# The input and forget gates of an mLSTM: float32 matmuls of 32 columns in four column groups instead of split matmuls of 100 columns

## The chip, the cores and the metric

The kernel runs on one core of a Trainium2 chip. The metric is the device time of one execution in microseconds (us); lower is better. The time before is the median of three runs.

## The reference, cut to what matters

One layer of a hybrid decoder: 1024 tokens of 1024 channels, three token mixers side by side on the same normalized input, and a gated MLP behind them. The change concerns the eight columns of the input projection that are the input and forget gates of the mLSTM (4 heads each), their biases, and what is made of them first.

```python
h = _rmsnorm(x, g_mix[l])
(sb_q, sb_k, sb_v, ml_q, ml_k, ml_v, ml_o, ml_i, ml_f, xa_q, gate_pre) = jnp.split(
    h @ w_in[l], offsets, axis=-1)
...
i_pre = (ml_i + ml_b_i[l]).astype(jnp.float32).transpose(0, 2, 1)
f_pre = (ml_f + ml_b_f[l]).astype(jnp.float32).transpose(0, 2, 1)
h_ml = _mlstm_chunkwise(
    _split_heads(ml_q, ML_HEADS).astype(jnp.float32),
    _split_heads(ml_k, ML_HEADS).astype(jnp.float32),
    _split_heads(ml_v, ML_HEADS).astype(jnp.float32), i_pre, f_pre)
...
log_f = jax.nn.log_sigmoid(f_pre)          # in _mlstm_chunkwise, chunks of 128 tokens
b = jnp.cumsum(lfc, axis=-1)
log_d = jnp.where(causal, b[..., :, None] - b[..., None, :] + ic[..., None, :], -jnp.inf)
```

## The kernel before, in words

Channels lie on the 128 partitions, tokens along the rows. The tokens are worked on as two halves of 512 (half 1 first); the kernel holds them in reverse order.

**The normalized input.** `x_norm` takes four float32 pages of x for one half (each page 128 x 1024: two channel tiles of 512 tokens), scales them into a tile `t` of the ring "U" (VectorE, L280), stores `t` to DRAM (L282), and splits it with `split` into a high and a low part: the high part rounded to the format fp32r by ScalarE (L129), the low part the rest (VectorE, L130). They are `hh[k]` and `hl[k]` for the 8 channel tiles k. All large projections use them in `mm3`, three fp32r matmuls for one product (L142 to L144), with weights split in the same way by `wsplit`.

**The gates.** Their weights `w_if` (128 x 8 x 8) are loaded into `wraw` (L295); a page `wif` of the ring "pg" is zeroed (L298), and the weights' high and low parts are put at columns 0 to 3, 32 to 35, 64 to 67 and 96 to 99 of each k (L300 to L303). `gates_if` (L460) takes for each half 16 matmuls of 100 output columns by 512 tokens: `wif` with `hh` (L464) and with `hl` (L465). It is a generator: one `next` makes one half. ScalarE and VectorE then add the low part and the bias for each gate and store 4 x 512 numbers (L468 to L471) to `if_d`.

**Order of the work.** The program is written out flat; a scheduler orders it by priority (the place in the program, moved ahead by `high_priority`) and by when operands and buffers are ready, and each engine then runs its list in order. The first 104 us go so: the memory's keys and values (`mem_mm`, L219), normalizing of half 1, query and key projection of the first pair of attention heads for half 1 (`chunks((1,))`, evicted by L367 to L370 and L374 to L379), the gates of half 1 (`next(gif)`), the value projection of token tiles 7 to 0 (`vals`, evicted by L488). Into the value projection are woven the sums of squares of half 0 (`x_stats`, L267 to L272; `rstd`, L158), its scale spread over the partitions (`spread`, L172), its normalizing, and the memory's keys (`mem_keys`, L227 to L231). The gates of half 0 come behind all token tiles. Then the attention begins (`sb_weights`, L404 and following), with `gate_rows` started in its third piece: it reads `if_d` as 32 rows (chunk and head) of 128 tokens for each gate (L531) and forms the running sums.

**Rings.** Buffers of one name are used in turn: "U" has 5 (squares, normalized pages, later the attention's weights), "pg" 16, "hf" 4, and the accumulators "pj", in which the projections and the gates are summed, 2.

**Attention's small matmuls** show how small shapes run: the transposes (L430, full width), and the application of the weights (L450), float32, 64 output columns by 128 tokens, written in turn to the partitions 0 to 63 and 64 to 127 of one accumulator. L805 sums squares with one output column, at partitions 0 and 64.

Of the kernel before, what the change touches and what calls it, by code (L numbers as in the profile page):

```python
# [10 lines left out]
F32 = mybir.dt.float32  # L11
F32R = mybir.dt.float32r
AF = mybir.ActivationFunctionType
ALU = mybir.AluOpType
# [4 lines left out]
P = 128  # L19
D = 1024  # L20
S = 1024
HALF = 512
KT = D // P
NMEM = 256
SBH, SBD = 8, 64
MLH, MLD = 4, 128
# [3 lines left out]
NCH = S // P  # L30
# [4 lines left out]
C_GMIX, C_GMEM, C_GFFN, C_CW, C_CB, C_GOUT, C_GQ, C_GK, C_FW, C_FB, C_BI, C_BF, C_END = (  # L35
    0, 8, 16, 24, 56, 64, 68, 69, 70, 202, 246, 247, 248)
# [6 lines left out]
def tile_hybrid_layer(ctx: ExitStack, tc: tile.TileContext, xT, memT, vecs, w_t, w_n, w_kv, w_if,  # L43
# [4 lines left out]
    nc = tc.nc  # L48
    const = ctx.enter_context(tc.tile_pool(name="const", bufs=1))
# [18 lines left out]
    def T(shape, tag, dt=F32, bufs=None):  # L68
        pool = {"mw": mlp, "mst": mlp, "px": late[0], "sx": late[0]}.get(tag, sb)
        return pool.tile(shape, dt, tag=tag, name=nm(tag), bufs=bufs or BUFS[tag])  # L70
# [4 lines left out]
    def half(dt=F32):  # L75
        return T([P, HALF], "hf", dt)
# [9 lines left out]
    def small(n, p=P):  # L86
        return T([p, n], "sm")

    def bank(tag):
        if tag in ("pj", "pv"):  # L90
            return ps.tile([P, HALF], F32, tag=tag, name=nm("ps_" + tag), bufs=2)
        if px1 is not None:
            if not spare.get(tag):
                t = two(tag)
                spare[tag] = [t[:, 1], t[:, 0]]
            return spare[tag].pop()
        return psx[0].tile([P, HALF], F32, tag=tag, name=nm("ps_" + tag), bufs=2)

    def dtile(shape, name):
        return dr.tile(shape, F32, tag=name, name=name)  # L100

    def hs(h):
        return slice(h * HALF, (h + 1) * HALF)
# [61 lines left out]
    def spread(r, nt):  # L165

        n = nt * P
        dg = half()
        for t in range(nt):
            nc.vector.tensor_scalar(dg[:, ts(t)], ident, r[:, t:t + 1], None, op0=ALU.mult)  # L170
        pb = bank("tr")
        nc.tensor.matmul(pb[:, :n], ones, dg[:, :n], start=True, stop=True)  # L172
        return pb[:, :n]
# [47 lines left out]
    def mem_keys(pm, rm):  # L221
        kns = []
        for m in range(2):
            ss = small(8)
            kn = half()
            for h in range(XAH):
                nc.scalar.activation(kn[:, ts(h)], pm[m][:, ts(h)], AF.Square, scale=rm[:, m:m + 1],  # L227
                                     accum_out=ss[:, h:h + 1])
            r = rstd_cols(ss[:, :XAH], XAH, XAD)
            for h in range(XAH):  # L230
                nc.vector.tensor_scalar(kn[:, ts(h)], pm[m][:, ts(h)], rm[:, m:m + 1], r[:, h:h + 1],  # L231
                                        op0=ALU.mult, op1=ALU.mult)
            kns.append(kn)
        return kns
# [40 lines left out]
    def x_norm(h, xp, rows):  # L275
        for j in range(4):
            t = wide()
            for k in (2 * j, 2 * j + 1):
                u = t[:, hs(k % 2)]
                nc.vector.scalar_tensor_tensor(u, xp[j][:, hs(k % 2)], col(C_GMIX + k), rows, op0=ALU.mult, op1=ALU.mult)  # L280
                split(u, hh[k][:, hs(h)], hl[k][:, hs(h)])
            nc.sync.dma_start(hn_d[h, j], t)  # L282

    pk, pv = [[bank(t) for _ in range(2)] for t in ("z", "pv")]
    xp = {0: [], 1: []}
# [4 lines left out]
    for b in range(1, 4):  # L290
        wk.append(mem_w(0, b))
        if b < 3:
            xp[1] += [x_page(1, i) for i in (2 * b - 2, 2 * b - 1)]
    wraw = T([P, KT, 8], "hf")
    nc.sync.dma_start(wraw, w_if.rearrange("p (k n) -> p k n", n=8))  # L295

    wif = T([P, KT, P], "pg", F32R)
    nc.vector.memset(wif.bitcast(F32), 0.0)  # L298
    for g in range(2):
        src = wraw[:, :, 4 * g:4 * g + 4]  # L300
        hi = wif[:, :, 32 * g:32 * g + 4]
        nc.scalar.activation(hi, src, AF.Copy)
        nc.vector.tensor_sub(wif[:, :, 64 + 32 * g:68 + 32 * g], src, hi.bitcast(F32))  # L303
    mem_mm(pk, wk[0], 0)
    mem_mm(pk, wk[1], 1)
    rm = mem_stats()
# [3 lines left out]
        wv.append(mem_w(1, b))  # L310
    r = rstd(x_stats(xp[1]), HALF)
    mem_mm(pv, wv[0], 0)
    x_norm(1, xp[1], spread(r, 4))
    for b in range(1, 4):
        mem_mm(pv, wv[b], b)

# [138 lines left out]
            store_y(0, p, rb // 4, pv)  # L455


    if_d = dtile([2, MLH, S], "if_d")

    def gates_if():  # L460
        for h in (1, 0):
            p = bank("pj")
            for k in range(KT):
                nc.tensor.matmul(p[:100], wif[:, k, :100], hh[k][:, hs(h)], start=(k == 0), stop=False)  # L464
                nc.tensor.matmul(p[:100], wif[:, k, :100], hl[k][:, hs(h)], start=False, stop=(k == KT - 1))  # L465
            for g in range(2):
                a, b = half(), half()
                nc.scalar.activation(a[:MLH], p[64 + 32 * g:68 + 32 * g], AF.Copy)  # L468
                nc.vector.scalar_tensor_tensor(b[:MLH], p[32 * g:32 * g + 4], vec[:MLH, C_BI + g:C_BI + g + 1],
                                               a[:MLH], op0=ALU.add, op1=ALU.add)  # L470
                nc.sync.dma_start(if_d[g, :, hs(h)], b[:MLH])  # L471
            yield

    st, chunks = sb_qk(0)
    early = []
# [2 lines left out]
        nc.sync.dma_start(raw, w_n[0, b])  # L478
        early.append(wsplit(None, "pg", raw=raw))
    xp[0] = [x_page(0, i) for i in range(4)]  # L480
    for _ in chunks((1,)):
        pass
    sbv = {}

# [2 lines left out]
            sbv[t // 2] = T([P, 2, HALF], "pg")  # L487
        nc.scalar.activation(sbv[t // 2][:, t % 2, :], p, AF.Copy)  # L488

    gif = gates_if()  # L490
    next(gif)
    vals = nat_chunks(0, ev_sbv, ws=early)
    for _ in range(2):
        next(vals)
# [3 lines left out]
    r = rstd(a, HALF)  # L498
    for _ in range(2):
        next(vals)  # L500
    x_norm(0, xp[0], spread(r, 4))
    for _ in range(3):
        next(vals)
    kn = mem_keys(pk, rm)
    mem_values(pv, rm)
    for _ in range(4):
        next(vals)
    mem_keys_out(kn)
    for _ in vals:
        pass  # L510
    for _ in gif:
        pass
    own = chunks((0,))

# [1 line left out]
    R = NCH * MLH  # L516
# [10 lines left out]
    def gate_rows():  # L527
        boxes = [T([P, MLH, P], "mw") for _ in range(2)]
        gi, gf, e, u, lu, bcur, r6, r7 = (boxes[i // 4][:R, i % 4] for i in range(8))
        for g, t in ((0, gi), (1, gf)):  # L530
            nc.sync.dma_start(t, if_d[g].rearrange("h (c t) -> c h t", t=P))  # L531

        nc.scalar.activation(e, gf, AF.Abs)
        nc.scalar.activation(e, e, AF.Exp, scale=-1.0)
        nc.vector.tensor_scalar(u, e, 1.0, None, op0=ALU.add)
        nc.scalar.activation(lu, u, AF.Ln)
        nc.vector.scalar_tensor_tensor(e, u, 1.0, e, op0=ALU.subtract, op1=ALU.subtract)
        nc.vector.reciprocal(u, u)
        nc.vector.tensor_mul(e, e, u)
        nc.vector.tensor_sub(lu, lu, e)  # L540
        nc.vector.scalar_tensor_tensor(bcur, gf, 0.0, lu, op0=ALU.min, op1=ALU.subtract)

        bcum = suffix(bcur, ALU.add, 0.0, r6)
        ga = gi
        nc.vector.tensor_sub(ga, gi, bcum)
        amax = suffix(ga, ALU.max, ga[:, P - 1:P], e)
        bl_d = dtile([2, R], "bl_d")
        nc.sync.dma_start(bl_d[0].rearrange("(r o) -> r o", o=1), bcum[:, 0:1])
        nc.sync.dma_start(bl_d[1].rearrange("(r o) -> r o", o=1), amax[:, 0:1])
        yield  # L550
        last = wide()[:MLH, :16]
        for g in range(2):
            nc.sync.dma_start(last[:, 8 * g:8 * g + 8].rearrange("h (c o) -> h c o", o=1),
                              bl_d[g].rearrange("(c h o) -> h c o", h=MLH, o=1))
        mp = small(8, MLH)
        nc.gpsimd.memset(mp, 0.0)
        for c in range(NCH - 1, 0, -1):
            nc.gpsimd.tensor_scalar(mp[:, c - 1:c], mp[:, c:c + 1], last[:, 8 + c:9 + c], last[:, c:c + 1],
                                    op0=ALU.max, op1=ALU.add)
        mp_d = dtile([NCH, MLH], "mp_d")  # L560
        nc.sync.dma_start(mp_d.rearrange("c (h o) -> h c o", o=1), mp.rearrange("h (c o) -> h c o", o=1))
        yield
        mprev = small(1, R)
        nc.sync.dma_start(mprev, mp_d.rearrange("c (h o) -> (c h) o", o=1))
        gm, ge, gw, gfl = gf, lu, bcur, u
        nc.gpsimd.tensor_scalar(gm, amax, mprev, -1.0, op0=ALU.max, op1=ALU.mult)
        nc.scalar.activation(ge, gm, AF.Exp, bias=mprev)
        nc.scalar.activation(gw, ga, AF.Exp, bias=gm[:, 0:1])
        nc.gpsimd.tensor_sub(gfl, gm, bcum)
        nc.scalar.activation(gfl, gfl, AF.Exp)  # L570
        nc.sync.dma_start(me_d[0], gm)
        nc.sync.dma_start(me_d[1], ge)
        yield
        pt = bank("tr")
        for i, t in enumerate((ga, gw, gfl)):
            nc.tensor.transpose(pt[:, i * R:(i + 1) * R], t, ident[:R, :R])
        nc.scalar.activation(cols.rearrange("p a r -> p (a r)"), pt[:, :3 * R], AF.Copy)
        yield
# [861 lines left out]
```

## Time and profile before

| | us |
|---|---|
| median of three runs | 1649.16 |
| lowest and highest | 1648.4 and 1650.76 |
| span of the profiled execution, first to last instruction | 1646.8 |

The profile is one execution; the engines are PE (TensorE matmul), PEld (its weight loads), DVE (VectorE), ACT (ScalarE), POOL (GpSimd) and SP (SyncE, which issues the DMAs). Its rows give that execution's span; its time with what lies around the span is not listed, so the 2.4 us between span and median stand for it. A row of the timeline has the start, the duration, the engine, the line in the kernel, the operation, the tiles written and read, the shapes (matmul: rows*columns of the weights, then the moving operand), how many instructions the row joins, and in brackets the idle time of the engine before it and what ended it. TensorE's granted clock is at full speed in all slices of the profile. A matmul's record lasts longer than the distance to the next, because matmuls are pipelined.

### The profile page before, as it was taken

The numbers are of one execution on the slowest core, as the hardware profiler recorded it, in microseconds if no ns is written. First come the engines' busy times: TensorE is split into PE (matmuls) and PEld (weight loads), VectorE is DVE, ScalarE is ACT, GpSimd is POOL, SyncE is SP. The second block draws the span as 40 slices with busy tenths as digits, with TensorE's granted clock in tenths as the row PEclk, the third lists the DMA queues.
The fourth block names the chain that finished last, engine by engine and source line by source line (L and its number), as shares of the span: only waits on it lengthen the run. The fifth ranks groups of instructions, "written<-read, shape, count | busy, mean of one in ns | idle before, by whom it ended". The sixth has DMA issues, their size and how long they took to land.

```text
span 1646.8 us, 21125 instructions
## 1 busy us (share of the span) xinstructions
PE 1630.4 (99%) x7911; PEld 1332.1 (81%) x7911; DVE 1210.1 (73%) x1683; ACT 827.9 (50%) x1276; POOL 92.4 (6%) x157
## 2 busy tenths in 40 slices
PE   8999999999999999999999999999999999999999
PEld 4788888887877888888788888788888888888887
DVE  5649888859764766766567658997888777799764
ACT  4557777545554454666322334655555545543431
POOL 1012222020000010100000000000000000000000
PEclk9999999999999999999999999999999999999999
DMA  8411111424324665434854453332222221586132
GB/s 295 154 55 34 39 40 65 140 86 150 125 100 139 197 192 167 135 101 136 282 185 159 137 184 127 108 110 71 77 77 85 98 87 51 173 312 243 43 126 82
DMA packets 96393, 212.68 MB, mean 129 GB/s; under 512 B 12432, under 2 KB 36240, under 8 KB 96292
## 3 DMA queue, kind: packets, MB, share of 16 engines
q1 hardware_dynamic: 96292, 211.35, 38.1%
q8 instruction: 62, 1.02, 0.2%
q14 instruction: 39, 0.32, 0.1%
HBM read 156.71 MB, written 54.61 MB: 128 GB/s over the span
## 4 chain that ended last, share of the span: by engine, by line
PE 90%; DVE 4%; DMA 3%; ACT 2%; issue 1%; SPq 0%; POOLq 0%; ACTq 0%; DVEq 0%
PE ps_pj L142 14%; PE ps_pj L143 14%; PE ps_pj L144 14%; PE ps_pv L142 6%; PE ps_pv L143 6%; PE ps_pv L144 6%; PE ps_tr L142 4%; PE ps_tr L144 4%; PE ps_tr L143 4%; PE ps_z L142 3%; PE ps_z L144 3%; PE ps_z L143 3%; PE ps_pv L450 2%; PE ps_tr L430 2%; PE ps_z L404 1%; PE ps_z L405 1%
## 5 line engine op out<-in xcount | busy, mean ns | idle before, releaser
L143 PE MATMUL ps_pj<-h,whi 128*128 128x512 f32 x624 | 244.2, 391 | 0.9 <-DVE h L130 0.9
L129 ACT ACTIVATE whi<-raw 128x512 fp32r<-128x512 f32 (+1 forms) x111 | 93.1, 839 | 172.3 <-PE ps_pj L143 62.6
L142 PE MATMUL ps_pj<-h,whi 128*128 128x512 f32 x416 | 165.7, 398 | 0.9 <-DVE U L1069 0.6
L142 PE MATMUL ps_pj<-pg,whi 128*128 128x512 f32 x396 | 154.7, 391 | 0.9 <-DVE pg L1067 0.9
L144 PE MATMUL ps_pj<-pg,wlo 128*128 128x512 f32 x376 | 146.5, 390 | 0.0
L143 PEld LDWEIGHTS ps_pj<-h,whi 128*128 128x128 f32 x624 | 117.3, 188 | 25.1 <-DVE h L130 1.8
L144 PE MATMUL ps_pj<-h,wlo 128*128 128x512 f32 x328 | 128.1, 391 | 0.0
L826 DVE SCALAR_TENSOR_TENSOR y<-U,vec,y 128x1023 f32<-128x1023 f32 x88 | 112.5, 1279 | 7.5 <-ACT y L824 7.5
L418 DVE TENSOR_TENSOR_SCAN U<-U 128x512 f32<-128x512 f32 (+3 forms) x96 | 92.7, 1007 | 20.6 <-POOL U L413 17.7
L142 PEld LDWEIGHTS ps_pj<-h,whi 128*128 128x128 f32 x416 | 78.2, 188 | 17.4 <-DVE U L1069 1.3
L142 PEld LDWEIGHTS ps_pj<-pg,whi 128*128 128x128 f32 x396 | 74.3, 188 | 17.2 <-DVE pg L1067 1.4
L130 DVE TENSOR_TENSOR wlo<-raw,whi 128x1024 fp32r<-128x1024 f32 x54 | 66.0, 1222 | 26.5 <-ACT whi L129 26.2
L144 PEld LDWEIGHTS ps_pj<-pg,wlo 128*128 128x128 f32 x376 | 70.6, 188 | 14.9 <-DVE wlo L130 0.3
L143 PE MATMUL ps_pj<-pg,whi 128*128 128x512 f32 x188 | 73.4, 390 | 0.0
L144 PEld LDWEIGHTS ps_pj<-h,wlo 128*128 128x128 f32 x328 | 61.6, 188 | 13.1
L129 ACT ACTIVATE whi<-pg 128x512 fp32r<-128x512 f32 (+1 forms) x46 | 35.3, 769 | 61.2 <-PE ps_pv L143 18.2
L824 ACT ACTIVATE y<-U,vec 128x1024 f32<-128x1024 f32 x44 | 54.6, 1241 | 17.5 <-DVE U L728 16.9
L144 PE MATMUL ps_pj<-h,whi 128*128 128x512 f32 x160 | 62.4, 390 | 0.0
L144 PE MATMUL ps_pv<-pg,wlo 128*128 128x512 f32 x150 | 58.4, 389 | 0.0
L130 DVE TENSOR_TENSOR wlo<-raw,wlo 128x512 fp32r<-128x512 f32 x55 | 37.8, 687 | 22.9 <-ACT wlo L129 22.7
L144 PE MATMUL ps_tr<-pg,wlo 128*128 128x512 f32 x140 | 54.5, 389 | 0.0
L407 ACT ACTIVATE U<-ps_z 128x1024 f32<-128x1024 f32 (+3 forms) x48 | 39.1, 814 | 27.6 <-PE ps_z L405 19.6
(465 smaller groups left out, 4331.6 us busy)
## 6 DMA issues: line engine op xcount, KB each, us to landing
raw<-in_w_t_dram SPq DMA_DIRECT2D x29, 512.0 KB
gate_d<-U SPq DMA_DIRECT2D x24, 512.0 KB
U<-gate_d SPq DMA_DIRECT2D x24, 512.0 KB
act_d<-y SPq DMA_DIRECT2D x22, 512.0 KB
pg<-in_w_t_dram SPq DMA_DIRECT2D x21, 512.0 KB
raw<-in_w_dn_dram SPq DMA_DIRECT2D x18, 512.0 KB
raw<-in_w_o_dram SPq DMA_DIRECT2D x16, 512.0 KB
h<-act_d SPq DMA_DIRECT2D x14, 512.0 KB
```

The lines of the kernel that those rows point to most:

```text
L129: nc.scalar.activation(hi, src, AF.Copy)
L130: (eng or nc.vector).tensor_sub(lo, src, hi.bitcast(F32))
L142: nc.tensor.matmul(out, lh, rh, start=start, stop=False, skip_group_check=more)
L143: nc.tensor.matmul(out, lh, rl, start=False, stop=False, skip_group_check=more)
L144: nc.tensor.matmul(out, ll, rh, start=False, stop=stop, skip_group_check=more)
L404: nc.tensor.matmul(z[:, a, :w], qs[a][:, ts(rb)], ks[a][:, c], start=True, stop=False)
L407: nc.scalar.activation(f[:, :, 1:w + 1], z[:, :, :w], AF.Sigmoid, scale=-0.125)
L418: nc.vector.tensor_tensor_scan(f[:, a, 1:w + 1], f[:, a, 1:w + 1], f[:, a, 1:w + 1], 1.0 if o == 0 else f[:, a, 0:1], op0=ALU.mult, op1=AL ...
L430: nc.tensor.transpose(pt[:, a, ts(j)], g[:, a, ts(j)], ident)
L450: nc.tensor.matmul(pv[64 * a:64 * a + 64, ts(rb % 4)], sbv[s // 2][:, s % 2, (2 * p + a) * 64:(2 * p + a + 1) * 64], wt[a][:, ts(j)], star ...
L824: nc.scalar.activation(out, u, AF.Identity, bias=bias, scale=taps[0])
L826: nc.vector.scalar_tensor_tensor(out[:, :S - s], u[:, s:], taps[s], out[:, :S - s], op0=ALU.mult, op1=ALU.add)
```

## The change

`x_norm` hands out its float32 tiles `t`, and the caller keeps them as `hf32`. `gates_if` is now a plain function of a half and these tiles: for each k, and for each quarter q of the half's 512 tokens, one float32 matmul of the weights (padded to 32 columns) with 128 tokens, put at the column group q of the array and so at the partitions 32q to 32q+31 of the accumulator. One copy by ScalarE evicts all four, and four stores of 8 x 128 numbers go to `if_d`, which now is laid out by chunk, gate and head. The weights' page, its split and its place in "pg" and "hf" go; the weights are a constant tile zeroed by GpSimd. The bias is added in `gate_rows`, where the rows are chunk and head, from a small tile loaded with a broadcast. The gates of half 1 move from behind the key projection to between query and key projection (after four steps of `first`), those of half 0 from the end of the value projection to behind its token tile 4.

```diff
@@ x_norm @@
             nc.sync.dma_start(hn_d[h, j], t)
+            yield t
@@ before mem_mm @@
-    wraw = T([P, KT, 8], "hf")
-    nc.sync.dma_start(wraw, w_if.rearrange("p (k n) -> p k n", n=8))
-
-    wif = T([P, KT, P], "pg", F32R)
-    nc.vector.memset(wif.bitcast(F32), 0.0)
-    for g in range(2):
-        src = wraw[:, :, 4 * g:4 * g + 4]
-        hi = wif[:, :, 32 * g:32 * g + 4]
-        nc.scalar.activation(hi, src, AF.Copy)
-        nc.vector.tensor_sub(wif[:, :, 64 + 32 * g:68 + 32 * g], src, hi.bitcast(F32))
+    wif = const.tile([P, KT, 32], F32, tag="wif", name="wif")
+    nc.gpsimd.memset(wif, 0.0)
+    nc.sync.dma_start(wif[:, :, :8], w_if.rearrange("p (k n) -> p k n", n=8))
...
-    x_norm(1, xp[1], spread(r, 4))
+    hf32 = list(x_norm(1, xp[1], spread(r, 4)))
@@ gates_if @@
-    if_d = dtile([2, MLH, S], "if_d")
-
-    def gates_if():
-        for h in (1, 0):
-            p = bank("pj")
-            for k in range(KT):
-                nc.tensor.matmul(p[:100], wif[:, k, :100], hh[k][:, hs(h)], start=(k == 0), stop=False)
-                nc.tensor.matmul(p[:100], wif[:, k, :100], hl[k][:, hs(h)], start=False, stop=(k == KT - 1))
-            for g in range(2):
-                a, b = half(), half()
-                nc.scalar.activation(a[:MLH], p[64 + 32 * g:68 + 32 * g], AF.Copy)
-                nc.vector.scalar_tensor_tensor(b[:MLH], p[32 * g:32 * g + 4], vec[:MLH, C_BI + g:C_BI + g + 1],
-                                               a[:MLH], op0=ALU.add, op1=ALU.add)
-                nc.sync.dma_start(if_d[g, :, hs(h)], b[:MLH])
-            yield
+    if_d = dtile([NCH, 2 * MLH, P], "if_d")
+
+    def gates_if(h, tiles):
+        p = bank("pj")
+        for k in range(KT):
+            for q in range(4):
+                nc.tensor.matmul(p[32 * q:32 * q + 32, :P], wif[:, k],
+                                 tiles[k // 2][:, (k % 2) * HALF + q * P:(k % 2) * HALF + (q + 1) * P],
+                                 start=(k == 0), stop=(k == KT - 1), tile_position=(0, 32 * q))
+        t = half()[:, :P]
+        nc.scalar.activation(t, p[:, :P], AF.Copy)
+        for q in range(4):
+            nc.sync.dma_start(if_d[4 * h + q], t[32 * q:32 * q + 2 * MLH])
@@ the order @@
-    for _ in chunks((1,)):
+    first = chunks((1,))
+    for _ in range(4):
+        next(first)
+    gates_if(1, hf32)
+    for _ in first:
         pass
...
-    gif = gates_if()
-    next(gif)
...
-    x_norm(0, xp[0], spread(r, 4))
+    hf32 = list(x_norm(0, xp[0], spread(r, 4)))
     for _ in range(3):
         next(vals)
+    gates_if(0, hf32)
     kn = mem_keys(pk, rm)
...
-    for _ in gif:
-        pass
@@ gate_rows @@
+        bias = small(2, R)
+        nc.sync.dma_start(bias, vecs[:MLH, C_BI:C_BI + 2].unsqueeze(0).to_broadcast([NCH, MLH, 2]))
         for g, t in ((0, gi), (1, gf)):
-            nc.sync.dma_start(t, if_d[g].rearrange("h (c t) -> c h t", t=P))
+            nc.sync.dma_start(t, if_d[:, 4 * g:4 * g + 4])
+            nc.gpsimd.tensor_scalar(t, t, bias[:, g:g + 1], None, op0=ALU.add)
```

In the prediction, a "half" is one call of the gates for 512 tokens, and a "step" the distance from one record's start to the next one's.

## The prediction

> **What bounds the kernel now.** First the page: busy times, then the chain that ended last.
>
> ```profile
> span 1646.8 us, 21125 instructions
> PE 1630.4 (99%) x7911; PEld 1332.1 (81%) x7911; DVE 1210.1 (73%) x1683; ACT 827.9 (50%) x1276; POOL 92.4 (6%) x157
> PE 90%; DVE 4%; DMA 3%; ACT 2%; issue 1%; SPq 0%; POOLq 0%; ACTq 0%; DVEq 0%
> ```
>
> TensorE (PE) is busy 99% of the span and is 90% of the chain, so time taken from PE leaves the total unless a wait takes its place. The second view is the timeline of PE around the two gate blocks (columns: start, duration, engine, line, tiles, shapes, count, idle before).
>
> ```profile
> 48.80 0.39 PE L144 MATMUL ps_pj<-h,wlo 128*128 128x512 f32 x1
> 49.24 0.44 PE L464 MATMUL ps_pj<-h,pg 128*100 128x512 f32 x1
> ...
> 53.71 0.47 PE L142 MATMUL ps_pj<-pg,h 128*128 128x512 f32 x1 [0.52 <-DVE pg L379]
> ...
> 99.91 0.39 PE L144 MATMUL ps_pj<-whi,h 128*128 128x512 f32 x1
> 100.14 0.39 PE L464 MATMUL ps_pj<-h,pg 128*100 128x512 f32 x1
> ...
> 103.76 0.22 PE L404 MATMUL ps_z<-pg,pg 128*128 128x128 f32 x1
> ```
>
> A record lasts 0.39 us but the next starts 0.23 us after it (99.91 to 100.14): they overlap, and the cost of one is its step. The second gate block holds PE from 100.14 to 103.76, 3.62 us for 16 matmuls, step 0.226. The first starts 0.21 us late (48.80 to 49.24 is 0.44, a step is 0.23), and 0.52 us of idle stand behind it: before 53.71, PE waits until VectorE (L379) has emptied the accumulator of the projection before. So the blocks and their waits cost 53.71 - 49.03 = 4.68 us and 3.62 us, 8.30 in all.
>
> **What is put in their place: 64 float32 matmuls of 32 output columns by 128 tokens.** No such row exists, so its price comes from three relatives.
>
> ```profile
> 68.36 1.02 PE L172 MATMUL ps_tr<-hf,ones 128*128 128x512 f32 x2
> ```
>
> ```profile
> 130.94 0.40 PE L144 MATMUL ps_pj<-h,wlo 128*128 128x512 f32 x1
> 131.26 0.66 PE L450 MATMUL ps_pv<-hf,pg 128*64 128x128 f32 x8
> 131.85 0.50 PE L404 MATMUL ps_z<-pg,pg 128*128 128x512 f32 x1
> ```
>
> ```profile
> 133.25 0.27 PE L450 MATMUL ps_pv<-y,pg 128*64 128x128 f32 x1
> ...
> 134.43 1.09 PE L430 MATMUL ps_tr<-ident,U 128*128 128x128 f32 x8
> ```
>
> ```profile
> 453.72 1.03 PE L805 MATMUL ps_tr<-y,ones 128*1 128x512 f32 x4
> ```
>
> L172 is one float32 matmul in the code and two records here (x2): float32 takes two passes, so the change brings 128 records. L430 is eight records of 128 columns, full width, one behind another; a single record of 128 columns is 0.27 long (133.25), so its step is (1.09 - 0.27) / 7 = 0.117 us. L450 is also 128 columns, but its output is 64 wide, two column groups in turn: eight records take 0.66 us, which is four rounds of two ((0.66 - 0.27) / 3 = 0.13), not eight in a row (1.09). L805 says the same of outputs one column wide in two groups: four records in 1.03 us, where L172's two alone take 1.02. Both passes of a matmul in one group thus lie beside both of the next group's. I take it that four groups do what two do: each of the 8 steps over k is two rounds of four, 16 rounds by 0.117 = 1.87 us a half. Going in costs 131.26 - 130.94 - 0.23 = 0.09, and coming out 131.85 - 131.26 - 4 x 0.117 = 0.12. **2.1 us a half.** The ends: 1.9 without the changes of mode; 64 x (0.66 - 0.27) / 7 = 3.5 us if no more than two run together; 64 x 0.117 = 7.5 us in single file. The two-group rows are the nearest, so I take the low end.
>
> ```profile
> 131.26 0.42 PEld L450 LDWEIGHTS ps_pv<-hf,pg 128*64 128x64 f32 x8 [0.36 <-issue]
> ```
>
> Here a rule speaks against the change. The Trainium skill, "TensorE: Matmul & The Clock Gate", section "Part 3: Packing small matmuls — row/col tiling", says that a weight load lies beside running matmuls only where the groups of rows differ; all four groups here use all 128 rows, so by it they come near single file, 7.5 us a half. This trace doesn't agree: L450's eight loads (same rows, other columns) take 0.42 us and lie wholly within its 0.66 us of matmuls.
>
> **First half: it moves ahead of the key projection and meets an accumulator.** The block now stands between the query half and the key half of the first projection. "pj" has two accumulators in turn: query A, gates B, key half A again. So the key half waits until A is emptied (L367 to L370), where before it went into B at once and only the gate block waited (the 0.21).
>
> ```profile
> 43.58 0.39 PE L142 MATMUL ps_pj<-h,whi 128*128 128x512 f32 x1
> ```
>
> ```profile
> 43.60 1.06 ACT L129 ACTIVATE whi<-raw 128x1024 fp32r<-128x1024 f32 x1 [2.78 <-PE ps_pj L143]
> 45.52 1.06 ACT L267 ACTIVATE U<-pg 128x1024 f32<-128x1024 f32 x1 [0.86 <-DMA pg<-in_xT_dram]
> 46.49 0.57 ACT L367 ACTIVATE pg<-ps_pj 64x512 fp32r<-64x512 f32 x1
> 47.08 0.59 ACT L368 ACTIVATE pg<-ps_pj 64x512 fp32r<-64x512 f32 x1
> ```
>
> ```profile
> 44.70 1.22 DVE L130 TENSOR_TENSOR wlo<-raw,whi 128x1024 fp32r<-128x1024 f32 x1 [1.82 <-ACT whi L129]
> 47.70 0.68 DVE L369 TENSOR_TENSOR pg<-ps_pj,pg 64x512 fp32r<-64x512 f32 x1 [1.78 <-ACT pg L368]
> 48.40 0.69 DVE L370 TENSOR_TENSOR pg<-ps_pj,pg 64x512 fp32r<-64x512 f32 x1
> ```
>
> ```profile
> 38.51 2.50 SPq L259 DMA_DIRECT2D pg<-in_xT_dram  x4
> ```
>
> The query half ends at 43.58, where the key half's first matmul stands; the gates would end at 45.68. As it stands A comes free at 48.40 + 0.69 = 49.09: ScalarE (ACT) first does a square (L267) that waited for a page of x. Those pages are fetched at 38.51, late, for want of "pg" buffers. The change takes the padded gate weights out of "pg", so I let the first page come one buffer sooner and its square be done before 43.6. Then L367 starts at 44.66, L368 ends at 45.84, VectorE's L130 ends at 45.92 and L369 and L370 at 47.3. The key half (43.58 to 49.03, 5.45 us) runs from 47.3 to 52.8, and the value projection's first matmul, which finds B empty, is at 52.8 instead of 53.71: **-0.9 us.** Of the 2.6 us saved in this half (4.68 - 2.1), 1.7 go into the wait. The other squares wait for "U" buffers until the gates have read them; PE asks for their sum 14 us after that, so this is hidden:
>
> ```profile
> 61.97 0.94 PE L158 MATMUL ps_tr<-ones,U 128*128 128x1 f32 x8
> ```
>
> The block's eviction is one ACT copy behind L368. Its four stores (two before) stand in SP's queue ahead only of weights that are split at 98.97 (below).
>
> **Second half: it moves from the end of the value projection to before token tile 3.**
>
> ```profile
> 77.20 0.39 PE L144 MATMUL ps_pj<-whi,h 128*128 128x512 f32 x1
> ```
>
> ```profile
> 70.54 1.05 DVE L231 TENSOR_SCALAR hf<-ps_z,sm,sm 128x128 f32<-128x128 f32 x3 [1.12 <-POOL U L411]
> 71.50 2.06 DVE L280 SCALAR_TENSOR_TENSOR U<-pg,vec,ps_tr 128x512 f32<-128x512 f32 x3
> ...
> 79.06 1.40 DVE L280 SCALAR_TENSOR_TENSOR U<-pg,vec,ps_tr 128x512 f32<-128x512 f32 x2
> ```
>
> ```profile
> 56.75 1.65 SPq L471 DMA_DIRECT2D if_d<-hf  x2
> ```
>
> ```profile
> 59.94 0.36 ACT L227 ACTIVATE hf<-ps_z,sm 128x128 f32<-128x128 f32 x1
> ```
>
> Token tile 4 ends at 77.42, and the block reads normalized pages whose last is written at 80.46 in this trace; tile 3 needs its first pages then, its last 5 us on, and so never waited. The block would stand until 80.46 and end at 80.9. But normalizing could start once L172 is done, 69.4, and starts at 71.50, behind the memory keys' L231; those came so late (L227 at 59.94) for "hf" buffers that the gates' stores (56.75) held. The change uses one such buffer a half instead of four, and none for the raw weights. I let the keys go ahead: the last page then comes near 78.4, and the block's eighth step, at 77.42 + 0.09 + 7 x 0.234 = 79.1, finds it. 3.62 becomes 2.1: **-1.5 us.**
>
> At its old place the block covered something.
>
> ```profile
> 98.97 1.06 ACT L129 ACTIVATE whi<-raw 128x1024 fp32r<-128x1024 f32 x1 [3.48 <-PE ps_pj L144]
> 100.07 1.23 DVE L130 TENSOR_TENSOR wlo<-raw,whi 128x1024 fp32r<-128x1024 f32 x1 [8.77 <-ACT whi L129]
> ```
>
> The next projection's low weights are ready at 101.30. With the block gone, four score matmuls of 128 columns (0.117 each, as in L430) and two long ones lead to the first that reads them, at 100.14 + 0.47 + 0.46 = 101.07: **+0.25 us.** The rest is off PE: the gate weights' split goes from ACT and VectorE, a memset and two bias additions come to GpSimd (6% busy), and the gate rows' input is there some 20 us sooner, which takes work from ACT at a time when PE doesn't wait. At nothing; with that cover gone, a few tenths.
>
> **Sum:** -0.9 - 1.5 + 0.25 = -2.15 us, span 1644.7. The runs' median, 1649.16, lies 2.4 us over the span; keeping that, **1647.0 us**, -0.13%. About 0.2%, 3.3 us, is what a measurement of this kernel can tell from no change.
>
> **Rivals and chances.**
> 1. The forecast, 0.38.
> 2. No buffer comes sooner, 0.22. The key half starts at 49.1, the value projection at 54.6 (+0.9); the second block ends at 80.9 (3.5 against 3.62, -0.1); with +0.25 that is +1.0: 1650.2. For it: the trace's own order. Against: the buffers that are freed.
> 3. No wait takes the gain, 0.18: the key half gets an accumulator by 45.7, the value projection starts at 51.1 (-2.6), then -1.5 and at worst +0.25: 1645.3, faster. It takes ACT and VectorE evicting the query half ahead of the split, which the trace doesn't.
> 4. Only two groups run together, 0.10: 3.5 us a half plus 0.2. The first ends at 47.3, inside the wait (-0.9), the second loses 0.1, and 0.25 comes on top: 1648.6.
> 5. The groups come in single file, 0.12, so the change doesn't do what it says; the rule on weight loads above leads here. 7.5 + 0.2 us a half: the key half starts at 51.3 and ends at 56.7 (+3.0), the second block costs 4.1 more, with 0.25 it is +7.3: 1656.5, slower. It passes 0.2% from 5.7 us a half, (5.7 - 0.2) / 64 = 0.086 us a record. L450 and L805 speak against it, but no row has four groups or 32 columns.
>
> Faster 0.18 (case 3), slower 0.12 (case 5), same 0.70. The range 1645.0 to 1651.2 holds cases 1 to 4 and leaves out 0.12 and a little.
>
> **What would show it.** Right: the gate matmuls, 64 records a half, in about 2 us each; a PE wait of 1 to 2 us before the key half's first matmul, ended by L370; no wait inside the second block; a small one after tile 0. Wrong: a gate record's step over 0.05 us; the key half starting before 46 or at 49; the square L267 still ahead of L367; PE idle in the second block; or a stage behind 130 us that differs by over 1 us, for which I have no term.

## The result, and the profile after

The changed kernel takes 1647.78 us (median of 21 runs, 1645.95 to 1649.39) where the kernel before, beside it, takes 1649.74 (21 runs). The ratio is 0.9984, interval 0.9978 to 0.9989: a gain of 2.0 us. The time lies 0.8 us above the forecast and inside the range. The number came out; most of what follows is about why the reasons did not.

The page of the changed kernel first: span and count, busy times, the chain by engine.

```profile
span 1646.1 us, 21299 instructions
PE 1627.0 (99%) x8007; PEld 1330.8 (81%) x8007; DVE 1206.7 (73%) x1676; ACT 822.2 (50%) x1269; POOL 92.5 (6%) x160
PE 85%; DVE 5%; DMA 2%; ACT 1%; issue 1%; POOL 0%; POOLq 0%; DVEq 0%; SPq 0%; ACTq 0%
```

PE is the bound as before, with 3.4 us less busy time and 0.7 us less span: part of what it no longer does has become waiting. The timeline of PE around both gate blocks and behind them says where.

```profile
44.21 0.39 PE L144 MATMUL ps_pj<-h,wlo 128*128 128x512 f32 x1
44.53 1.96 PE L458 MATMUL ps_pj<-U,wif 128*32 128x128 f32 x64
47.88 0.50 PE L142 MATMUL ps_pj<-h,whi 128*128 128x512 f32 x1 [1.39 <-ACT hf L462]
...
53.45 0.39 PE L142 MATMUL ps_pj<-pg,h 128*128 128x512 f32 x1
...
76.84 0.39 PE L144 MATMUL ps_pj<-whi,h 128*128 128x512 f32 x1
77.16 1.95 PE L458 MATMUL ps_pj<-U,wif 128*32 128x128 f32 x64
79.04 0.50 PE L142 MATMUL ps_pj<-pg,h 128*128 128x512 f32 x1
...
90.06 0.60 PE L240 MATMUL ps_tr<-ident,hf 128*128 128x128 f32 x4
...
91.43 0.39 PE L143 MATMUL ps_pj<-pg,h 128*128 128x512 f32 x1
93.47 0.66 PE L240 MATMUL ps_tr<-ident,hf 128*128 128x128 f32 x4 [1.65 <-DVE hf L242]
...
104.42 0.40 PE L143 MATMUL ps_pj<-h,whi 128*128 128x512 f32 x1
104.96 0.50 PE L144 MATMUL ps_pj<-h,wlo 128*128 128x512 f32 x1
...
122.62 0.39 PE L144 MATMUL ps_pj<-h,wlo 128*128 128x512 f32 x1
123.69 0.50 PE L399 MATMUL ps_z<-pg,pg 128*128 128x512 f32 x1 [0.68 <-DVE pg L372]
```

A gate block is 64 records in 1.96 us; less the last record's 0.27 that is 15 rounds of four, 0.113 us each. So four column groups do run together. From the end of the query half to the value projection it is now 53.45 - 44.44 = 9.01 us (53.71 - 43.58 = 10.13 before): -1.12. A second profile of the kernel before takes 53.99 - 44.37 = 9.62 us there, so half a microsecond of this differs between executions of one kernel. The second block costs 79.04 - 77.07 = 1.97 us where 3.62 stood: -1.65. Then come waits that were not there. Before the memory keys' second transposes (L240) the next start comes 93.47 - 91.43 = 2.04 us later where a step is 0.23: 1.81 lost (the 1.65 in the bracket counts from the end of the record). Before the first low weights it is 0.31 (104.42 to 104.96 is 0.54). Together -1.12 - 1.65 + 1.81 + 0.31 = -0.65 us. Right behind the low weights 0.4 more is lost up to 109 us: from the first record of line 144 there to the fifth it is 3.59 us, 3.21 before. The wait of 0.84 at 122.62 (1.07 to the next start) is no further loss: the attention's first matmuls stand in another order than before, and ahead of and behind this stretch, at 118 and at 137 us, the changed kernel is 0.23 and 0.15 us ahead.

That can be followed through the run. In the table, a kernel's n-th record of line 144 (of 2108) is timed from its first, and the same figure of the first profile of before is taken off; the first one itself stands between 38.51 and 39.45 us over all profiles, the kernel before alone at 38.56 and 39.34. n = 110, 241, 801, 1001 and the last are at 137, 322, 744, 884 and 1643 us in before; at each of them PE has the same work behind it in all kernels, the gates apart.

| us against before at | 137 | 322 | 744 | 884 | end |
|---|---|---|---|---|---|
| changed kernel | -0.15 | +0.03 | +0.09 | -1.99 | -1.86 |
| changed kernel, second profile | -0.05 | -0.15 | -0.06 | -1.85 | -1.77 |
| before, second profile | -0.52 | -0.41 | -0.08 | +0.65 | +1.34 |

So around the gates nothing is won in the end: the differences there, 0.15 us at most, are smaller than the 0.4 to 0.5 us between the two profiles of before. What is won comes between 744 and 884 us, in a stage whose instructions on PE are the same, in the same order, in both kernels.

### The profile page after: what moved, and what is told of

Same layout as the page of the kernel before. It is cut to its first block, busy times and chain, and to the rows that moved or that the text cites. A ratio compares the mean times of both kernels' runs of the same rounds, so it can differ in the third digit from the quotient of the medians.

```text
span 1646.1 us, 21299 instructions
## 1 busy us (share of the span) xinstructions
PE 1627.0 (99%) x8007; PEld 1330.8 (81%) x8007; DVE 1206.7 (73%) x1676; ACT 822.2 (50%) x1269; POOL 92.5 (6%) x160
## 4 chain that ended last, share of the span: by engine, by line
PE 85%; DVE 5%; DMA 2%; ACT 1%; issue 1%; POOL 0%; POOLq 0%; DVEq 0%; SPq 0%; ACTq 0%
PE ps_pj L142 13%; PE ps_pj L144 13%; PE ps_pj L143 13%; PE ps_pv L143 6%; PE ps_pv L144 6%; PE ps_pv L142 6%; PE ps_tr L144 4%; PE ps_tr L143 4%; PE ps_tr L142 4%; PE ps_z L142 3%; PE ps_z L144 3%; PE ps_z L143 3%; PE ps_pv L444 2%; PE ps_tr L424 1%; DVE U L412 1%
```

## The experiments

The kernels of each batch ran on one chip beside the kernel before; "against before" is the table's figure above. They are told by question. The first theory for the small result was that the new waits give the gain back; its rival, that slack later in the run takes up anything saved.

**The two large waits.** The key half's: half 1 is summed in an accumulator of the ring "tr", which the transposes use.

```diff
-    def gates_if(h, tiles):
-        p = bank("pj")
+    def gates_if(h, tiles, tag="pj"):
+        p = bank(tag)
...
-    gates_if(1, hf32)
+    gates_if(1, hf32, "tr")
```

> Only the accumulator of half 1's gates changes: one of the ring tr instead of pj. Theory A (the change saves about 2.8 us of PE around the gates; two new waits give most of it back: 1.4 us before the key half, which takes over the gates' accumulator, and 1.8 us before the second pair of key transposes, which takes over the accumulator of the first): the key half follows the gates with no wait, and, because the tr halves are now paired otherwise, the second transposes follow without a wait. 3.0 us faster than the changed kernel, ratio to before 0.9966. Theory B (the work between 105 and 320 us is held by ACT and VectorE, which take up what PE saves before it): both waits go from the profile, but the time stays at 0.998 to 0.999 of before.

The transposes': half 0 goes back behind the value projection, and with it everything that its input releases.

```diff
-    gates_if(0, hf32)
     kn = mem_keys(pk, rm)
...
+    gates_if(0, hf32)
```

> Only the place of half 0's gates changes: back behind the value projection. Theory A: the gate rows come late again, VectorE empties the first key transposes at once, the wait of 1.8 us before the second ones falls to under 0.2, the small wait (0.3) for the next projection's low weights goes, the key half's 1.4 us stay. 2.0 us faster than the changed kernel, ratio 0.9972. Rival: the wait comes from the pairing of the tr accumulators alone, not from the gate rows in VectorE's queue; then it stays near 1.8 and the ratio is 0.998. Theory B: 0.998 to 0.999 whatever the waits do.

Or the transposes are emptied by another engine, and half 0 stays:

```diff
-            nc.vector.tensor_scalar(kt, pt, gqk, None, op0=ALU.mult)
+            nc.scalar.activation(kt, pt, AF.Copy, scale=gqk)
```

> Only the engine that empties the key transposes changes: ACT instead of VectorE (L242). Theory A: the first transposes are emptied within 1 us, as VectorE's queue (gate rows, a step of which waits for ACT's Ln) no longer stands before it; the second transposes wait under 0.3 us instead of 1.8; 1.6 us faster than the changed kernel, ratio 0.9974. Rival: what is late is something else (the stores, the keys): the wait stays and the ratio is 0.998. Theory B: wait gone, ratio 0.998 to 0.999.

First and second edit together, twice, and first and third:

> Half 1's gates in tr and half 0's behind the value projection. Theory A: none of the three waits is left (1.4, 1.8, 0.3); 3.4 us faster than the changed kernel, ratio 0.9964, at most 0.3 us better than the accumulator alone. Theory B: 0.998 to 0.999.

> The kernel with both places mended (half 1 into the accumulator of the transposes, half 0 back behind the value projection), unchanged, once more. If its waits are gone for good: ratio 0.995 to 0.9965 again and -4.6 us up to 322 us, within 0.3 us.

> The changed kernel with two edits: half 1 into the accumulator of the transposes, and the first key transposes emptied by ScalarE instead of VectorE; half 0 stays at its new place. If the two waits add up as terms of their own (-0.88 and -2.52 us up to 322 us against the change): -3.4 us there, with the 0.3 us for the low weights and the 0.85 us in the attention's first pieces still there; that leaves 1.2 us between it and the kernel with half 0 put back, and the new place of half 0 would have no worth of its own. If the new place is worth something once the waits are gone: below -4.6.

What holds the transposes is in VectorE's own timeline of the changed kernel. L531 to L541 are the gate rows, L242 is the eviction of the first transposes, which ended at 90.06 + 0.60:

```profile
88.42 0.37 DVE L531 TENSOR_SCALAR mw<-mw 32x128 f32<-32x128 f32 x1 [0.54 <-ACT mw L530]
88.83 0.28 DVE L533 SCALAR_TENSOR_TENSOR mw<-mw 32x128 f32<-32x128 f32 x1
90.04 0.94 DVE L534 RECIPROCAL mw<-mw 32x128 f32<-32x128 f32 x1 [0.94 <-ACT mw L532]
...
92.47 0.28 DVE L541 TENSOR_TENSOR mw<-mw,mw 32x128 f32<-32x128 f32 x1
92.68 0.73 DVE L242 TENSOR_SCALAR hf<-ps_tr,gqk 128x512 f32<-128x512 f32 x1
```

and what the gate rows wait for is in ScalarE's, a table load ahead of the logarithm L532:

```profile
88.41 1.28 ACT L532 ACT_TABLE_LOAD   x1
89.70 0.31 ACT L532 ACTIVATE mw<-mw 32x128 f32<-32x128 f32 x1
```

With half 0 late (VectorE, second edit) the same eviction starts as soon as its input is there:

```profile
87.46 0.75 DVE L242 TENSOR_SCALAR hf<-ps_tr,gqk 128x512 f32<-128x512 f32 x1 [6.95 <-PE ps_tr L240]
```

and on ScalarE (third edit) it passes the gate rows:

```profile
90.27 0.68 ACT L242 ACTIVATE hf<-ps_tr,gqk 128x512 f32<-128x512 f32 x1
```

PE's second transposes with the first, the second and the third edit, one fence each:

```profile
88.40 0.60 PE L240 MATMUL ps_tr<-ident,hf 128*128 128x128 f32 x4
...
91.83 0.65 PE L240 MATMUL ps_tr<-ident,hf 128*128 128x128 f32 x4 [1.67 <-DVE hf L242]
```

```profile
86.82 0.60 PE L240 MATMUL ps_tr<-ident,hf 128*128 128x128 f32 x4
...
88.42 0.60 PE L240 MATMUL ps_tr<-ident,hf 128*128 128x128 f32 x4
```

```profile
89.58 0.60 PE L240 MATMUL ps_tr<-ident,hf 128*128 128x128 f32 x4
...
91.01 0.66 PE L240 MATMUL ps_tr<-ident,hf 128*128 128x128 f32 x4
```

| kernel | median us | ratio to before, interval | against before at 137 | at 322 | end |
|---|---|---|---|---|---|
| half 1 in "tr" | 1647.61 | 0.9978 (0.9969 to 0.9987) | -1.00 | -0.85 | -2.61 |
| half 0 late | 1643.97 | 0.9961 (0.9949 to 0.9974) | -3.42 | -3.71 | -5.14 |
| L242 on ScalarE | 1645.18 | 0.9966 (0.9953 to 0.9978) | -2.21 | -2.49 | -5.25 |
| "tr" and half 0 late | 1643.85 | 0.9958 (0.9946 to 0.9971) | -4.18 | -4.64 | -6.77 |
| the same once more | 1642.89 | 0.9959 (0.9946 to 0.9972) | -4.26 | -4.58 | -6.82 |
| "tr" and L242 on ScalarE | 1644.26 | 0.9964 (0.9951 to 0.9976) | -3.38 | -3.82 | -4.53 |

The first edit removes the key half's wait, but is worth 0.85 us at 137 us, not the 3 I expected: I had let the transposes' wait go with it, and that wait stayed (1.67 us). The second and third edits are worth 3.3 and 2.1 us there. Of this, 0.6 and 0.3 us stand at 55 us already, where neither edit has acted: in the same code the key half waited 0.77 and 1.07 us instead of 1.39, as the page of x came sooner. The rest, 2.7 and 1.8 us (2.0 and 1.6 expected), is what the edits brought. Both remove the transposes' wait, each in a different way, so the cause is the place of L242 in VectorE's queue. The theory that slack later takes up whatever is saved falls: no saving over the changed kernel at 137 us shrinks by more than 0.6 us up to the end, and three grow. What remains between the two kernels with "tr" at 137 us, 4.2 - 3.4 = 0.8 us (1.2 expected), is about what half 0 costs at its new place: 0.3 for the low weights and the 0.4 right behind them, which the kernels with half 0 late don't have. So moving half 0 ahead has no worth of its own. By the traces "tr" with half 0 late is the best version, 6.8 us under the first profile of before in both profiles of it; the runs' times put it ahead of both kernels, but don't tell it from half 0 late alone (1643.85 and 1643.97 in one batch).

**What makes four groups run together.** Only the order of the gate matmuls is changed; first the loops are swapped:

```diff
-        for k in range(KT):
-            for q in range(4):
+        for q in range(4):
+            for k in range(KT):
```

> The changed kernel with the two loops of the gate matmuls swapped: all eight steps over k of one column group, then the next group. The work is the same and only the neighbours in the order change. Theory 1 (four groups run together because neighbours in the order lie in different column groups): now single file, 64 records by 0.112 to 0.117 us = 7.2 to 7.5 us a half instead of 1.96. The first block then ends near 52 instead of 46.5, and the key half starts there instead of at 47.88 (+4.2); the second block is 5.3 us longer; +9.5 us against the changed kernel, a ratio to the kernel before of 1.0042. Theory 2 (a record of 32 columns is simply cheaper, in any order): 1.96 us a half and 0.9984.

Then pairs:

```diff
-        for k in range(KT):
-            for q in range(4):
+        for k, q in [(k, q + j) for q in (0, 2) for k in range(KT) for j in range(2)]:
+            if True:
```

> The changed kernel with its gate matmuls in pairs: for two column groups all eight steps over k, then for the other two. Theory 1 (what runs together is what stands beside each other in the order): 32 rounds by 0.112 us = 3.6 us a half. The first ends at 48.2, 0.3 us behind the wait that is there already, the second is 1.6 us longer: +1.9 us against the changed kernel, ratio 0.9995. If the core looks further ahead in the order than the next record: 2.0 us a half and 0.9984.

PE's timeline of the swapped kernel, then of the one in pairs, then the gate line's own view in the swapped one (duration of a record: lowest, median, highest in ns), and last the swapped kernel's timeline once more, asked for up to 45.8 us, so that only the first 12 records of the first group are joined:

```profile
44.56 5.96 PE L458 MATMUL ps_pj<-U,wif 128*32 128x128 f32 x64
50.88 0.50 PE L142 MATMUL ps_pj<-h,whi 128*128 128x512 f32 x1 [0.37 <-ACT hf L462]
```

```profile
43.88 3.29 PE L458 MATMUL ps_pj<-U,wif 128*32 128x128 f32 x64
47.54 0.50 PE L142 MATMUL ps_pj<-h,whi 128*128 128x512 f32 x1 [0.38 <-ACT hf L462]
```

```profile
L458 PEld LDWEIGHTS ps_pj<-U,wif x128: 106/110/110, 44.6 to 85.8; 128*32 128x32 f32 x128
L458 PE MATMUL ps_pj<-U,wif x128: 272/273/297, 44.6 to 85.9; 128*32 128x128 f32 x128
```

```profile
44.56 1.50 PE L458 MATMUL ps_pj<-U,wif 128*32 128x128 f32 x12
```

The same 64 records take 5.96 us in single file ((5.96 - 0.27) / 63 = 0.090 us a record), 3.29 in pairs ((3.29 - 0.27) / 31 = 0.097 a pair), 1.96 in fours (0.113 a four), with the same durations of records and loads. The gain is thus one of order: neighbours in the instruction stream must lie in different column groups. These averages hide a simpler picture. The record starts in the traces are 0.109 us apart within one group ((1.50 - 0.27) / 11 gives 0.11), and in the pairs and the fours, too, a round starts 0.109 us after the one before, its records 0.007 us apart; only the first round takes 0.13. What makes single file and pairs shorter than their count of rounds is the change from one group, or pair, to the next: there, in single file, eight records start within 0.36 us, as if the tail of one lay beside the head of the next. The swapped kernel takes 1655.64 us, ratio 1.0030 (1.0018 to 1.0042), +6.8 us against before at 137 us; the one in pairs 1649.36, 0.9996 (0.9987 to 1.0005), +1.5. Single file is cheaper than I expected (5.96 us a half for 7.2 to 7.5), mostly by that overlap, so the first costs 7.0 us over the change and not 9.5; the pairs come 0.3 us a half under the 3.6 expected.

**Places or matmuls.** The new matmuls at the old places:

```diff
-    for _ in range(4):
-        next(first)
-    gates_if(1, hf32)
     for _ in first:
         pass
+    gates_if(1, hf32)
...
-    gates_if(0, hf32)
     kn = mem_keys(pk, rm)
...
+    gates_if(0, hf32)
```

> The new float32 gate matmuls at the old places: half 1 behind the key half, half 0 behind the whole value projection. Theory A (the cheaper blocks are worth what no wait takes back): in the first half the value projection still waits for the accumulator that VectorE empties after the key half, so the 2.6 us saved there turn into a longer wait (0.52 becomes some 2.5 to 3 us) and bring nothing; the second half brings 1.65 less 0.3 for the low weights; the key transposes don't wait. About -1.4 us up to 322 us, against +0.03 for the change and -3.7 with only half 0 put back. Theory C (the new places bring nothing, the matmuls bring all): as good as the kernel with half 0 put back, -3.7 there.

And the old fp32r block (weights' split, 100 columns, evictions, bias) at the new places:

```diff
     for _ in range(4):
         next(first)
-    gates_if(1, hf32)
+    next(gif)
...
     for _ in range(3):
         next(vals)
-    gates_if(0, hf32)
+    next(gif)
```

> The old fp32r gate matmuls at the new places: half 1 between query and key half, half 0 behind token tile 4. Theory A: the first block (3.6 us) ends close to where the key half's accumulator comes free, so the key half starts at about 48 as with the change and the value projection 0.5 to 0.9 us earlier than before; the second block costs what it did (3.62) or more, as it needs the split pages, which are later than the float32 ones; the gate rows go ahead of the key transposes and cost them 1.6 to 1.8 us. Sum 0 to +2 us against the kernel before, ratio 1.000 to 1.0015. Theory C (the places bring nothing and take nothing): ratio 1.000, and the key transposes don't wait.

PE's timeline at the old places with new matmuls, then at the new places with old ones:

```profile
49.96 1.95 PE L458 MATMUL ps_pj<-U,wif 128*32 128x128 f32 x64 [0.39 <-DVE pg L364]
53.58 0.47 PE L142 MATMUL ps_pj<-pg,h 128*128 128x512 f32 x1 [1.67 <-DVE pg L373]
```

```profile
50.02 0.47 PE L142 MATMUL ps_pj<-h,whi 128*128 128x512 f32 x1 [1.88 <-DVE pg L370]
...
93.67 0.60 PE L240 MATMUL ps_tr<-ident,hf 128*128 128x128 f32 x4
...
97.29 0.66 PE L240 MATMUL ps_tr<-ident,hf 128*128 128x128 f32 x4 [1.87 <-DVE hf L242]
```

At the old places the saving of the first half turns into longer waits on both sides of the block, as expected (-0.53 us at 65 us, where the second profile of before stands at -0.51); the second half brings 1.5: -2.1 us at 137 us and -2.45 at 322 (expected -1.4: the low weights' 0.3 did not come, since the block still covers them). 1646.37 us, 0.9975 (0.9965 to 0.9985). The order alone, with the old block, costs +3.7 us at 137 us: 1654.23 us, 1.0023 (1.0013 to 1.0032), worse than I expected, as the key half here waits for the query's accumulator until 50.02 (+0.9 at the value projection) and every one of the later waits is there too. The matmuls bring time, the places take it.

**The late gain.** Kernel before and changed kernel once more, unchanged:

> The kernel before, unchanged, for a second profile of it. Theory J (the 2 us that the change and nearly all variants gain on the first profile of before between its 744 and 883 us, where the programs are the same, are waits that fall differently in each execution): this profile, too, differs there from the first one by 1 us or more, without any edit. Theory K (the gain there belongs to the change): this profile shows the same waits there as the first one, 2.0 us in all, and differs by less than 0.5 us.

> The changed kernel, unchanged, for a second profile of it. Up to 322 us of the first profile of before it stands where the first profile of the change did, within 0.3 us of it (+0.03 there), counted from the first projection's third matmul; between 744 and 883 us theory J expects another amount than the -2.0 us of the first, theory K the same. Ratio 0.998 to 0.999.

1650.54 us, 0.9999 (0.9990 to 1.0007), and 1647.27, 0.9984 (0.9975 to 0.9992). The stretch from 744 to 884 us by engine (length, then busy time and instructions of PE, PEld, DVE, ACT and POOL, then clock, DMA share, GB/s): before, its second profile, the changed kernel, its second profile, and the old block at the new places.

```profile
744.00:884.00 140.00, 138.45 (x628) 112.05 (x627) 84.81 (x130) 49.21 (x78) 1.92 (x1) 1.00 0.61 199
```

```profile
744.00:884.00 140.00, 137.33 (x624) 111.67 (x623) 84.08 (x128) 49.35 (x78) 1.92 (x1) 1.00 0.60 198
```

```profile
744.00:884.00 140.00, 139.47 (x637) 114.13 (x636) 86.41 (x131) 49.91 (x79) 1.92 (x1) 1.00 0.60 202
```

```profile
744.00:884.00 140.00, 139.51 (x635) 113.64 (x635) 85.85 (x131) 50.12 (x79) 1.92 (x1) 1.00 0.60 200
```

```profile
744.00:884.00 140.00, 138.57 (x632) 112.12 (x631) 85.79 (x133) 52.80 (x84) 1.92 (x1) 1.00 0.59 199
```

PE stands idle there for 1.55 and 2.67 us before, 0.53 and 0.49 after, and 1.43 with the old block. In the nine other profiles, all with the new matmuls, it is 0 to 0.95. By the table's records the second profile of before loses 0.7 us more in this stretch than the first (one theory expected 1 us or more, the other under 0.5), the old block at the new places gains 0.4, and the eleven profiles with the new matmuls gain 1.0 to 2.7. So the waits vary from execution to execution, but not freely: the profiles with the new matmuls keep apart from the three with the old. One part goes wholly with the matmuls. ScalarE's timeline of before, then of the changed kernel, at the split of a page of y:

```profile
753.60 1.06 ACT L129 ACTIVATE pg<-raw 128x1024 fp32r<-128x1024 f32 x1 [1.13 <-DMA raw<-y_d]
```

```profile
753.93 1.06 ACT L129 ACTIVATE pg<-raw 128x1024 fp32r<-128x1024 f32 x1 [0.49 <-DVE wlo L130]
```

In the three profiles with the old matmuls the split waits for the page's transfer (1.13, 1.64 and 1.72 us) and starts 4.5 to 5.1 us after the transfer is issued; in all eleven with the new ones the page is there, at most 3.9 us after its issue, and the split waits for VectorE. The attention's next steps and their transposes (L1020) stand behind it: by records the new matmuls gain 0.42 to 0.45 us here, where the other two old profiles lose 0.5 and 0.6. A later wait of the same kind, where the merge (L1067) stands until the first page of MLP gates has come from DRAM, doesn't divide them so: 2.13 and 2.28 us before, 1.21 with the old block, 1.69 and 0.77 after, 1.99 with half 0 late.

Why the pages come earlier with the new matmuls isn't shown. Old and new block differ ahead of it in the "pg" page of the weights, a constant tile, the evictions and their stores, and no run separates these. With three profiles of the old matmuls, how much of the 2 us belongs to them and how much to the execution isn't shown either. That part of the gain stays open.

## Why the prediction's number held and its steps did not

- **The price of the matmuls: right.** 2.1 us a half was forecast, 1.97 is what the second block costs, and 0.11 more goes into the slower first step behind it (0.34 us for 0.23); a round of four is 0.113 us on average (0.117 forecast). Rivals 4 and 5 fall. The rule that rival 5 drew from the Trainium skill ("TensorE: Matmul & The Clock Gate", "Part 3: Packing small matmuls — row/col tiling"), that a load lies beside running matmuls only where the groups of rows differ, does not hold here: all four groups use the same 128 rows, and a record with its 0.110 us load takes 0.113 / 4 = 0.028 us. Even in single file, where all records of a group use the same rows, a record's step is 0.109 us, no longer than its load.
- **First half, -0.9 forecast, -1.12 measured (-0.6 against the second profile of before); the reasons fell.** The step was "I let the first page come one buffer sooner and its square be done before 43.6". The pages were not fetched sooner (SP's timeline of the changed kernel: 0.06 us ahead of the first record of line 144, 0.05 before), and the square L267 was still ahead (ScalarE's):

```profile
39.37 2.38 SPq L259 DMA_DIRECT2D pg<-in_xT_dram  x4
```

```profile
46.60 1.06 ACT L267 ACTIVATE U<-pg 128x1024 f32<-128x1024 f32 x1 [1.08 <-DMA pg<-in_xT_dram]
47.56 0.26 ACT L462 ACTIVATE hf<-ps_pj 128x128 f32<-128x128 f32 x1
47.72 0.58 ACT L361 ACTIVATE pg<-ps_pj 64x512 fp32r<-64x512 f32 x1
```

  And the key half did not wait for the query's accumulator but took the gates' own, free at 47.82 when L462 had read it; the block's last record ended at 46.49, but L462 stands behind the square, which waited for its page. The two errors cancel by luck: it started at 47.88, forecast 47.3, in a profile whose first record of line 144 comes 0.87 us later. So rival 2's condition, no buffer sooner, held without its 49.1, and rival 3's free accumulator did not come by 45.7. In the run of the old block at the new places the key half does wait for the query's (L370, 50.02), so which of the two it takes was not to be read from the ring alone.
- **Second half, -1.5 forecast, -1.65 measured; again with the wrong reason.** "I let the keys go ahead": they went later. In VectorE's timeline the normalizing starts as soon as PE has spread the scale, and the last page is written at 76.64 + 1.40 = 78.04, before the block's last steps; the memory keys' L231 come at 82.23.

```profile
69.06 2.06 DVE L280 SCALAR_TENSOR_TENSOR U<-pg,vec,ps_tr 128x512 f32<-128x512 f32 x3 [4.31 <-PE ps_tr L172]
...
76.64 1.40 DVE L280 SCALAR_TENSOR_TENSOR U<-pg,vec,ps_tr 128x512 f32<-128x512 f32 x2
...
82.23 1.36 DVE L231 TENSOR_SCALAR hf<-ps_z,sm,sm 128x128 f32<-128x128 f32 x4 [1.12 <-POOL sm L150]
```

- **Cover lost, +0.25 forecast: right**, 0.31.
- **"At nothing", with a few tenths if the cover is gone: the step that failed.** I counted the gate rows' earlier start as work taken from ScalarE and asked only whether PE waits for the gate rows. I did not ask what stands behind them in VectorE's queue: L242, for which PE waits 1.65 us, 1.81 by steps. With the 0.4 us behind the low weights, whose cause wasn't followed further, this is 2.2 us where I had put nothing, most of the 2.8 that both halves saved.
- **"A stage behind 130 us that differs by over 1 us, for which I have no term": it does**, by about 2 us between 744 and 884. It stands for the gain that the gates themselves did not bring. So 1647.0 was right to 0.8 us by luck: a missed cost and a missed gain are of the same size.

## What to carry to other kernels

The small matmuls here came to a third of their time in single file (1.96 us for 5.96) only with neighbours in the instruction order that lie in other column groups, so the loop over groups goes inside. When work is moved ahead, follow its results too: what becomes ready sooner enters in-order queues sooner, and whatever then stands behind it there is late. A number that comes out is no proof of its reasons: compare the traces stage by stage, with a second profile of the kernel before, ahead of crediting a change with a gain.

## What the runs showed of the hardware

- A round of float32 records of 128 columns with 32 output columns starts 0.109 us after the one before, whether it has one, two or four column groups (swapped kernel, pairs, changed kernel), against 0.117 for the full-width transposes of the prediction's rows. Over a whole half the averages are 0.090, 0.049 and 0.028 us a record, shorter in single file and pairs by what happens at the change from one group, or pair, to the next.
- The switch into the column groups costs the 0.09 us forecast: 44.53 - 44.21 - 0.23.
- The first projection's first record of line 144 moves by 0.9 us between profiles (38.51 to 39.45), and by 0.8 us between the two of the kernel before (38.56 and 39.34).
